# Moving weight-block preparation between stages, and two base blocks into a spare buffer, in a soft-routing expert matmul

## The chip, the cores and the metric

The kernel runs on one core of a Trainium2 chip. The metric is device time in microseconds (us) of one execution; lower is better. The core has TensorE (PE, matmuls; its weight loads are listed as PEld), VectorE (DVE), ScalarE (ACT), GpSimd (POOL) and SyncE (SP). In this kernel SyncE, ScalarE and GpSimd each issue DMA transfers from a queue of their own, and every engine works through its instructions in program order.

## The reference

Every token's row of x goes through all eight experts, and the results are summed with the softmax of the router's logits as weights:

```python
batch, seq, hidden, n_experts, expert_hidden = 16, 512, 512, 8, 2048
probs = softmax(router_logits)                     # (16, 512, 8)
for e in range(n_experts):
    output += probs[:, :, e:e+1] * np.matmul(x, expert_weights[e])
```

Inputs and output are float32. Seen as one matmul, the left matrix has 8192 rows (tokens) and 8 x 512 = 4096 columns, each x row scaled by its eight probabilities; the right matrix is the eight experts' weights under each other, 4096 x 2048.

## The kernel before, in words

The big matmul is done by Strassen's method in Winograd's form, at two levels everywhere and at a third level in part. At the outer level the tokens are taken in pairs of blocks of 256 rows (16 pairs, q = 0 to 15), the 4096 products' length in two halves (experts 0 to 3 and 4 to 7), and the 2048 output columns in two halves. So the weights are four blocks 11, 12, 21, 22, and seven kinds of product (P1 to P7) replace eight. Their right operands are 11 (P1), 21 (P2), T1 (P5), T2 (P6), T3 (P7), T4 (P4) and 22 (P3), where T1 to T4 are sums and differences of the four blocks. Each block has four parts, named by a pair kn: (0,0), (1,0), (1,1) and the "odd" part (0,1).

Each product is a smaller Winograd product of seven steps, and a step is one **slot**: 8 matmuls of 128 x 128 by 128 x 512, 1.73 us at full clock. A **stage** holds one product (7 slots) or two (14 slots, taken in turn). There are 56 stages. Where a stage has third-level work ("third"), the first four slots are replaced by 56 small matmuls, and the last two slots (12 and 13) of the stage before are held back and run inside it. Counting the program's matmuls against the trace gives the stages' starts:

| stages | what | first stage starts at, us |
|---|---|---|
| 0 to 6 | P1, q = 2 to 15, two a stage, all third | 38.9 |
| 7 to 14 | P2, two a stage; 8 to 12 third | 209.2 (stage 12: 323.4; 13: 350.3; 14: 374.4) |
| 15 | P5 for q = 0 and 1 | 398.6 |
| 16 | P6 for q = 0, alone | 422.8 |
| 17 to 30 | P6 for q and P5 for q + 1 | 438.9 (24.2 a stage) |
| 31 to 47 | P7, P4 | 777.3 |
| 48 to 55 | P3; 49 to 54 third | 1188.3 |

Before stage 0 the P1 products of q = 0 and 1 are done directly. Stage 4 starts at 130.7 and stage 5 at 154.0.

What an engine does beside the matmuls is placed by hooks: `at(stage, slot, make)` runs `make` just before that slot. DVE's longer work (left operands, sums of weights) is not run at once but put into one first-in-first-out list by `later(cost, make)`; `slack()` takes from it after each slot as far as a clock of planned costs allows, and `need(task)` takes everything up to that task. The left operands of stage s + 1 join this list after slot 0 of stage s. Results of matmul steps in PSUM are taken out by DVE or ACT right behind each step, in the same program order. In a third stage, two short DVE sums (line 735) stand between two groups of small matmuls, and TensorE waits for them.

Left operands are `z` tiles: x transposed (`xT`) times probabilities (`pT`). In P1 the x blocks of stages 3 to 6 are cast by GpSimd into tile `u` two stages ahead (`x_room`, `XBlock.begin`) and then transposed by SyncE's DMA (`XBlock.finish`).

Tiles come from pools: 15 buffers of 8 KB a partition for weights (`w`), 13 of 2 KB for half blocks of 128 x 512 float32 (`h`), 1 of 4 KB for `u`, 8 for `z`. A tile can be had only when the last use of its buffer is over, a DMA out of it included.

The parts that the change touches:

- `wedge(kn, e)` (one half e of part kn): GpSimd casts the half parts of 12 and 22 from float32 into one tile, DVE makes T1 = 11 - 12 and T2 = 22 + T1 of it, 128 x 2048 float16 each, and GpSimd sends both to DRAM for P5 and P6. There are six. `wedge_at(stage, slot, kn, e, then, apart)` places the first cast, the second `apart` slots later, and at `then` the two sums join DVE's list.
- The odd part: `cast_odd` casts it for 12, 11, 22 and 21 at the listed slots (two halves each); `odd_t` makes T1, T3 and T2 of it in place, three DVE sums of 128 x 4096, from (12, 5) on; `odd_t4` makes T4 from (15, 4) on, when the casts of 21 have landed.
- `Base`: P2 and P6 add to blocks that P1 left in DRAM (`kept`). `fetch(tn)` takes an `h` tile and loads one 128 x 512 block by SyncE. In P6 the result of P5 is then subtracted from it (`joined`, from slot 12 of the stage before), the matmul results are added in place, and GpSimd writes it out.

Of the kernel before, what the change touches and what calls it, by code (L numbers as in the profile page):

```python
# [31 lines left out]
def kernel(  # L32
# [8 lines left out]
    P = 128  # L41
    f16 = mybir.dt.float16
    f32 = mybir.dt.float32
    ADD, SUB, MUL = mybir.AluOpType.add, mybir.AluOpType.subtract, mybir.AluOpType.mult
# [5 lines left out]
    C = H // P  # L50
    HE = E // 2
    NB = 512
# [12 lines left out]
    zpool = ctx.enter_context(tc.tile_pool(name="zpool", bufs=8))  # L65
# [8 lines left out]
    def h_tile(shape, dtype):  # L74
        return hpool.tile(shape, dtype, name="h", tag="h")

    def half():
        return h_tile([P, NB], f32)
# [21 lines left out]
    def note(i):  # L100
        last[i.ins.engine] = i.ins
        if ordered[0]:
            tc.keep_in_program_order(i)

    def dve(i):
        last[i.ins.engine] = i.ins
        tc.keep_in_program_order(i)
# [3 lines left out]
    def tt(o, a, b, op):  # L111
        dve(nc.vector.tensor_tensor(out=o, in0=a, in1=b, op=op))  # L112
# [9 lines left out]
    def sp(o, i):  # L122
        note(nc.sync.dma_start(out=o, in_=i))

    def pool(o, i, **how):
        note(nc.gpsimd.dma_start(out=o, in_=i, **how))  # L126
# [32 lines left out]
    def kept_w(what, kn):  # L159
        if (what, kn) not in stored:  # L160
            stored[what, kn] = dram.tile([C, P, 2, NB] if what in TWOS else [P, K8, NB], f16, name="wd")
        kept_t = stored[what, kn]
        return kept_t.rearrange("a p b n -> p a b n") if what in TWOS else kept_t
# [122 lines left out]
    def third_weights(w, t, i):  # L286
        block = lambda k, n: w[:, ds(k * C, C), COLS[n]]
        x, y = ((block(0, 1), block(0, 0)), (block(1, 1), t[:, 0]), (block(1, 1), block(0, 1)),
                (block(1, 0), t[:, 1]))[i]
        tt(t[:, i], x, y, SUB)  # L290

    def new_t():
        return wpool.tile([P, 4, C, HQ], f16, name="t", tag="w")
# [116 lines left out]
    def need(task):  # L410
        if task is not None and not task.done:
            flush(task)
            clock["pe"] = max(clock["pe"], clock["dve"])

    def later(cost, make, first=False):
        t = Task(cost, make)
        (queue.appendleft if first else queue.append)(t)
        return t
# [144 lines left out]
    class Operand:  # L563
# [5 lines left out]
        def fetch(self):  # L569
            self.t = wpool.tile([P, 2, K8, HQ], f16, name="o", tag="w")  # L570
            note(nc.scalar.dma_start(out=self.t, in_=self.source))
# [78 lines left out]
    class Split:  # L650
# [10 lines left out]
        def make(self, p, i):  # L661
            if i == 0:
                self.t[p] = new_t()
            third_weights(self.right.op(p), self.t[p], i)
# [60 lines left out]
    def out_rows(q, odd, cols, tn):  # L725
        t, n = tn
        return out_f[ds((2 * q + odd) * HQ + t * HP, HP), ds(cols * NH + n * NB, NB)]

    def to_out(q, odd, cols, **how):
        return lambda tn, o: pool(out_rows(q, odd, cols, tn), o, **how)  # L730

    class Base:
# [2 lines left out]
        def __init__(self, source):  # L735
            self.source, self.t = source, {}

        def fetch(self, tn):
            self.t[tn] = half()
            sp(self.t[tn], self.source(tn))  # L740

        def __call__(self, tn):
# [8 lines left out]
    def at(stage, slot, make):  # L751
        hooks.setdefault((stage, slot), []).append(make)

    def add(*products):
        stages.append(products)
        return len(stages) - 1
# [4 lines left out]
    lefts, xs, ps_, bases = {}, {}, {}, {}  # L761
# [35 lines left out]
    def kept_rows(q):  # L797
        return lambda tn: kept[q][tn[1], ds(tn[0] * HP, HP), :]

    def product(r, q, **how):  # L800
        left, loads = left_of(r, q)
        lefts[r, q] = left
        p = None
        if r == 1:
            def sink(tn, o):
                pool(kept_rows(q)(tn), o)
            p = Product(right[1], left, sink)
        elif r == 2:
            if q >= 14:
                base = products[1, q].o.__getitem__  # L810
            else:
                base = bases[2, q] = Base(kept_rows(q))
            p = Product(right[2], left, to_out(q, 0, 0), base)
        elif r == 5:
            bases[6, q] = m1 = Base(kept_rows(q))
            m1.task = {}

            p = Product(right[5], left, to_out(q, 1, 0))
        elif r == 6:
            m1 = bases[6, q]  # L820

            def base(tn):
                need(m1.task[tn])
                return m1.t[tn]
            p = Product(right[6], left, to_out(q, 0, 1), base)
            if q in KEEP:
                left.kept = dram.tile([P, 2, K8, HQ], f16, name=f"kept_left_{q}")
        elif r == 7:
            if q < 14:
                base = bases[7, q] = Base(lambda tn: out_rows(q, 0, 1, tn))  # L830
            else:
                base = products[6, q].o.__getitem__
            p = Product(right[7], left, to_out(q, 1, 1), base)
        elif r == 4:
            p = Product(right[4], left, to_out(q, 1, 0, accum_op=ADD), products[7, q].o.__getitem__)
        else:
            p = Product(right[3], left, to_out(q, 0, 1, accum_op=ADD), **how)
        p.loads = loads
        products[r, q] = p
        return p  # L840
# [107 lines left out]
        for n in range(end, len(slots)):  # L948
            held.append(lambda n=n: one(n))

    def fetch_at(stage, slot, base, *tns):
        for tn in tns:
            at(stage, slot, lambda tn=tn: base.fetch(tn))


    for q in range(2, 16, 2):
# [1 line left out]
    forget(*range(0, 28, 2))  # L958
    rest = [14, 15] + list(range(14))
    for i in range(0, 16, 2):  # L960
        k = add(product(2, rest[i]), product(2, rest[i + 1]))
        for slot, tn in zip((8, 10, 12, 13), INNER):
            for q in rest[i:i + 2]:
                if q < 14:
                    fetch_at(k if tn == (1, 0) else k - 1, 3 if tn == (1, 0) else slot, bases[2, q], tn)
    xs.clear()
    k5 = add(product(5, 0), product(5, 1))
    add(product(6, 0))
# [20 lines left out]
    def joined(q, tn):  # L989
        m1 = bases[6, q]  # L990
        m1.task[tn] = later(0.61, lambda: tt(m1.t[tn], m1.t[tn], products[5, q].o[tn], SUB), True)

    for q in range(16):
        k = k5 + 1 + q
        duo = len(stages[k - 1]) == 2
        for slot, tn in zip((2, 4, 6, 8) if duo else (1, 2, 3, 4), INNER):
            fetch_at(k - 1, slot, bases[6, q], tn)
        for tn, where in zip(INNER, ((k - 1, 12), (k - 1, 13), (k - 1, 13), (k, 3)) if duo
                             else ((k - 1, 5), (k - 1, 6), (k - 1, 6), (k, 3))):
            at(*where, lambda q=q, tn=tn: joined(q, tn))  # L1000
        if q < 14:
            for slot, tn in zip((7, 9, 11, 17), INNER):
                fetch_at(k7 + q + 1 + slot // 14, slot % 14, bases[7, q], tn)
# [37 lines left out]
    b21, t1, t2, t3 = {}, {}, {}, {}  # L1041
# [11 lines left out]
    def sums_at(stage, slot, r, of, ps):  # L1053
        def go():
            if right[r].w is None:
                right[r].sums = right[r].build(of)
            for p in ps:
                right[r].queue_sum(right[r].sums, p)
        at(stage, slot, go)
# [1 line left out]
    sums_at(6, 6, 2, b21, (6,))  # L1061
    sums_at(6, 8, 2, b21, (7,))
    sums_at(6, 12, 2, b21, (4,))
    WEDGES = ((1,3,(1,11),4),(2,3,(2,11),4),(3,2,(3,9),4),(6,2,(6,11),4),(7,8,(8,7),4),(8,9,(9,9),4))
    for i, (kn, e) in enumerate((kn, e) for kn in ((0, 0), (1, 0), (1, 1)) for e in range(2)):
        wedge_at(*WEDGES[i][:2], kn, e, *WEDGES[i][2:])

# [3 lines left out]
    ODD = 0, 1  # L1071


    made = {}

    def cast_odd(q, e):
        if e == 0:
            made[q] = new_w()
        cast_w(q, ODD, e, made[q][:, ds(e * C, C), :])

    def odd_t():

        def make1():
            t1[ODD] = made[11]
            tt(t1[ODD], made[11], made[12], SUB)

        def make3():
            tt(made[12], made[22], made[12], SUB)
            pool(kept_w("t3", ODD), made.pop(12))

        def make2():
            t2[ODD] = made[22]
            tt(t2[ODD], made[22], t1[ODD], ADD)
        for make in (make1, make3, make2):
            later(2.2, make)

    def odd_t4():
        def make():
# [14 lines left out]
        return one(4, b[1, 0], b[1, 0], b[1, 1]) if all_ else sixth  # L1113

    last2 = k5 - 1
    for stage, slot, q, e in ((9, 9, 12, 0), (9, 13, 12, 1), (10, 4, 11, 0), (10, 9, 11, 1), (11, 2, 22, 0), (11, 7, 22, 1), (14, 8, 21, 0), (14, 12, 21, 1)):
        at(stage, slot, lambda q=q, e=e: cast_odd(q, e))
    at(12,5, odd_t)
    for i, kn in enumerate(((0, 0), (1, 1), (1, 0))):
        fetch_at_w(*(((11,8),(12,4),(13,0)))[i], t1, "t1", kn)  # L1120
# [229 lines left out]
```

## Time and profile before

| | us |
|---|---|
| median of 3 runs | 1365.48 |
| lowest, highest | 1364.68, 1372.43 |
| the profiled execution | 1371.11 |
| its span, first to last instruction | 1369.4 |
| TensorE busy | 1358.2 (99%) |
| DVE busy | 1154.2 (84%) |
| DMA queue of GpSimd, share of 16 engines | 56.5% |
| DMA queue of SyncE | 33.1% |
| DMA queue of ACT | 7.9% |

The profile is of one execution, which took 5.6 us more than the median. In the timeline a row is a run of like instructions: start, time to the end of the last, engine, line, what is written from what, how many, and in brackets how long the engine was idle before it and what ended that. In a table of stretches, PEclk is the share of its full clock that TensorE was granted, and the DMA share is the time of all packets over 16 engines' time; packets overlap, so it can pass 1.

### The profile page before, as it was taken

Reading aid. Unit: us, or ns where it says so; the run is one execution under the profiler, and the core shown is the slowest. Engines: PE = TensorE matmul, PEld = TensorE weight load, DVE = VectorE, ACT = ScalarE, POOL = GpSimd, SP = SyncE. Lnnn points to the kernel's source line nnn. Section 1 sums busy time; section 2 is a strip of 40 time slices with the busy share of each in tenths; the row PEclk is TensorE's granted clock in tenths of the full one; section 3 lists DMA queues with packets and bytes.
Section 4 is the critical chain, followed back from the end, with each engine's and each line's share of the span. In section 5 each row is a group of like instructions: output and inputs, shape, how many; then the busy total and the mean of one; then the engine's idle time right before and its main releaser. Section 6 shows DMA issues by size and latency. Waiting matters only on the chain.

```text
span 1369.4 us, 18641 instructions
## 1 busy us (share of the span) xinstructions
PE 1358.2 (99%) x6825; PEld 666.0 (49%) x6825; DVE 1154.2 (84%) x1429; ACT 204.5 (15%) x390; POOL 415.7 (30%) x650
## 2 busy tenths in 40 slices
PE   9999999999999999999999999999999999999998
PEld 4555555555444444444444444444444444456564
DVE  7987489988999888888878988888889797898873
ACT  3332221111011111111111100000000000123221
POOL 3133332231213243343323222232332422233232
PEclk9999999999999999999999999999999999999999
DMA  9999998999898999999999988889898979999896
GB/s 194 220 268 225 279 218 260 275 301 358 262 326 269 276 298 301 316 290 321 281 297 313 397 301 223 211 239 209 229 251 227 246 200 292 294 226 240 198 212 109
DMA packets 198811, 357.74 MB, mean 261 GB/s; under 512 B 53312, under 2 KB 90432, under 8 KB 194368
## 3 DMA queue, kind: packets, MB, share of 16 engines
q0 software_dynamic: 90448, 183.02, 56.5%
q1 hardware_dynamic: 100208, 133.56, 33.1%
q10 hardware_dynamic: 8064, 39.99, 7.9%
q8 instruction: 53, 0.87, 0.2%
q14 instruction: 38, 0.31, 0.1%
HBM read 218.92 MB, written 167.97 MB: 283 GB/s over the span
## 4 chain that ended last, share of the span: by engine, by line
PE 88%; issue 4%; DMA 3%; DVE 3%; POOL 1%; SPq 0%; POOLq 0%; ACT 0%; DVEq 0%
PE ps L132 88%; DMA out_dram<-h 2%; POOL out_dram L126 1%; DVE z L112 1%; DMA xT<-u 1%; DMA w<-in_expert_weights_dram 1%; DMA pT<-p_dram 1%; DVE h L112 0%; DVE t L112 0%; DVE u L112 0%; DVE s L112 0%; DVE d L112 0%; POOL wd L126 0%; DVE w L112 0%; POOL w L126 0%
## 5 line engine op out<-in xcount | busy, mean ns | idle before, releaser
L132 PE MATMUL ps<-w,z 128*128 128x512 f16 x5128 | 1094.5, 373 | 0.3 <-DMA w<-in_expert_weights_dram 0.3
L132 PEld LDWEIGHTS <-z 128*128 128x128 f16 x5272 | 516.1, 98 | 578.4 <-issue 5.1
L126 POOL DMA_DIRECT2D out_dram<-h x380 | 249.3, 662 | 710.2 <-ACT h L638 344.4
L112 DVE TENSOR_TENSOR h<-ps,h 128x512 f32<-128x512 f32 x415 | 283.4, 687 | 127.5 <-PE ps L132 114.5
L112 DVE TENSOR_TENSOR z<-xT,pT 128x2048 f16<-128x2048 f16 x216 | 261.5, 1218 | 23.8 <-DMA kept_left<-z 7.7
L132 PE MATMUL ps<-w,d 128*128 128x512 f16 x880 | 201.4, 382 | 2.2 <-DVE ps L112 2.2
L132 PEld LDWEIGHTS <-d 128*128 128x128 f16 x880 | 86.6, 98 | 103.8 <-issue 5.1
L112 DVE TENSOR_TENSOR z<-z,d 128x2048 f16<-128x2048 f16 x110 | 132.2, 1217 | 0.0
L112 DVE TENSOR_TENSOR w<-w 128x1024 f16<-128x1024 f16 (+2 forms) x100 | 108.1, 1091 | 13.6 <-DMA w<-in_expert_weights_dram 8.6
L638 ACT COPY h<-ps 128x512 f32<-128x512 f32 x64 | 37.5, 586 | 509.4 <-PE ps L132 461.6
L627 ACT COPY h<-ps 128x512 f32<-128x512 f32 x90 | 52.8, 587 | 273.8 <-PE ps L132 244.5
L112 DVE TENSOR_TENSOR d<-z 128x1024 f16<-128x1024 f16 x110 | 74.1, 687 | 1.5
L126 POOL DMA_DIRECT2D w<-in_expert_weights_dram x77 | 57.1, 753 | 44.4 <-DMA wd<-w 31.0
L624 ACT COPY h<-ps 128x512 f32<-128x512 f32 x90 | 51.6, 590 | 121.7 <-PE ps L132 97.5
L126 POOL DMA_DIRECT2D wd<-w x90 | 53.1, 605 | 43.9 <-DVE w L112 29.1
L126 POOL DMA_DIRECT2D kept<-h x56 | 30.9, 552 | 114.0 <-ACT h L627 85.0
L132 PEld LDWEIGHTS <-s 128*128 128x128 f16 x576 | 56.4, 98 | 10.6 <-issue 0.4
L132 PE MATMUL ps<-t,s 128*128 128x256 f16 x432 | 58.9, 273 | 0.1
L112 DVE TENSOR_TENSOR ps<-ps,d 128x256 f32<-128x256 f32 x72 | 30.2, 430 | 25.6 <-PE ps L132 25.5
L112 DVE TENSOR_TENSOR ps<-ps,h 128x512 f32<-128x512 f32 (+1 forms) x66 | 45.3, 688 | 4.7 <-PE ps L132 4.7
L112 DVE TENSOR_TENSOR h<-h 128x512 f32<-128x512 f32 (+2 forms) x69 | 45.1, 676 | 3.6 <-DMA out_dram<-h 3.5
L112 DVE TENSOR_TENSOR u<-xT,pT 128x2048 f16<-128x2048 f16 x38 | 46.3, 1218 | 0.0
(61 smaller groups left out, 354.8 us busy)
## 6 DMA issues: line engine op xcount, KB each, us to landing
out_dram<-h POOLq DMA_DIRECT2D x380, 256.0 KB, 7.3
pT<-p_dram SPq DMA_DIRECT2D x125, 256.0 KB, 7.0
h<-kept SPq DMA_DIRECT2D x120, 256.0 KB, 8.4
w<-wd ACTq DMA_DIRECT2D x25, 1024.0 KB, 10.6
xT<-x SPq DMA_DIRECT2D x77, 256.0 KB, 7.5
wd<-w POOLq DMA_DIRECT2D x76, 256.0 KB, 6.3
w<-in_expert_weights_dram POOLq DMA_DIRECT2D x35, 512.0 KB, 11.4
h<-out_dram SPq DMA_DIRECT2D x60, 256.0 KB, 5.4
```

Source lines behind the costliest of these rows:

```text
L112: dve(nc.vector.tensor_tensor(out=o, in0=a, in1=b, op=op))
L126: note(nc.gpsimd.dma_start(out=o, in_=i, **how))
L132: note(nc.tensor.matmul(ps, z, w, start=start, stop=stop, skip_group_check=True))
L624: act(nc.scalar.copy(o[tn], q if p == 5 else x))
L627: act(nc.scalar.copy(o[TN[p]], b if p == 2 else x))
L638: act(nc.scalar.copy(o[tn], b))
```

## The change

Four things change.

- The six wedges move. Old and new places (first cast; the sums join the list), in the order of the parts: (1,3; 1,11) to (0,4; 0,12); (2,3; 2,11) to (1,4; 1,12); (3,2; 3,9) to (6,3; 6,12); (6,2; 6,11) to (7,6; 7,13); (7,8; 8,7) to (8,6; 8,13); (8,9; 9,9) to (9,6; 9,13). The second cast stays four slots behind the first.
- The casts of the odd part of 21 go from slots 8 and 12 of stage 14 to slots 3 and 8.
- The three sums of `odd_t` are done in two halves each, six DVE operations of 128 x 2048 in the place of three of 128 x 4096.
- In stages 8, 10 and 12 of P2 the blocks (0,0) of both products, and in P6 for odd q from 1 to 13 the blocks (0,0) and (1,1), are loaded into the two halves of a tile of `u`'s buffer rather than into two `h` tiles.

```diff
-        def fetch(self, tn):
-            self.t[tn] = half()
+        def fetch(self, tn, pair=None):
+            if pair is None:
+                self.t[tn] = half()
+            else:
+                if not pair:
+                    two = zpool.tile([P, 2, NB], f32, name="r", tag="u", bufs=1)
+                    pair += [two[:, i] for i in range(2)]
+                self.t[tn] = pair.pop()
             sp(self.t[tn], self.source(tn))
...
     for i in range(0, 16, 2):
+        pair = [] if i // 2 in (1,3,5) else None
         k = add(product(2, rest[i]), product(2, rest[i + 1]))
...
-                    fetch_at(k if tn == (1, 0) else k - 1, 3 if tn == (1, 0) else slot, bases[2, q], tn)
+                    fetch_at(k if tn == (1, 0) else k - 1, 3 if tn == (1, 0) else slot, bases[2, q], tn,
+                             pair=pair if tn == (0, 0) else None)
...
         duo = len(stages[k - 1]) == 2
+        pair = [] if q in range(1, 14, 2) else None
         for slot, tn in zip((2, 4, 6, 8) if duo else (1, 2, 3, 4), INNER):
-            fetch_at(k - 1, slot, bases[6, q], tn)
+            fetch_at(k - 1, slot, bases[6, q], tn, pair=pair if tn in ((0, 0), (1, 1)) else None)
...
-    WEDGES = ((1,3,(1,11),4),(2,3,(2,11),4),(3,2,(3,9),4),(6,2,(6,11),4),(7,8,(8,7),4),(8,9,(9,9),4))
+    WEDGES = ((0,4,(0,12),4),(1,4,(1,12),4),(6,3,(6,12),4),(7,6,(7,13),4),(8,6,(8,13),4),(9,6,(9,13),4))
...
     def odd_t():
-
-        def make1():
+        halves = [ds(e * C, C) for e in range(2)]
+
+        def make1(h):
             t1[ODD] = made[11]
-            tt(t1[ODD], made[11], made[12], SUB)
-
-        def make3():
-            tt(made[12], made[22], made[12], SUB)
-            pool(kept_w("t3", ODD), made.pop(12))
-
-        def make2():
+            tt(t1[ODD][:, h], made[11][:, h], made[12][:, h], SUB)
+
+        def make3(h):
+            tt(made[12][:, h], made[22][:, h], made[12][:, h], SUB)
+            if h is halves[1]:
+                pool(kept_w("t3", ODD), made.pop(12))
+
+        def make2(h):
             t2[ODD] = made[22]
-            tt(t2[ODD], made[22], t1[ODD], ADD)
+            tt(t2[ODD][:, h], made[22][:, h], t1[ODD][:, h], ADD)
         for make in (make1, make3, make2):
-            later(2.2, make)
+            for h in halves:
+                later(1.14, lambda make=make, h=h: make(h))
...
-    for stage, slot, q, e in (..., (14, 8, 21, 0), (14, 12, 21, 1)):
+    for stage, slot, q, e in (...,(14,3,21,0),(14,8,21,1)):
```

More of the change, by code (lines that the diff above doesn't have):

```diff
@@ L949, in run, with fetch_at @@
             held.append(lambda n=n: one(n))
-    def fetch_at(stage, slot, base, *tns):
+    def fetch_at(stage, slot, base, *tns, pair=None):
         for tn in tns:
-            at(stage, slot, lambda tn=tn: base.fetch(tn))
+            at(stage, slot, lambda tn=tn: base.fetch(tn, pair))
     for q in range(2, 16, 2):
@@ L1115 @@
     last2 = k5 - 1
-    for stage, slot, q, e in ((9, 9, 12, 0), (9, 13, 12, 1), (10, 4, 11, 0), (10, 9, 11, 1), (11, 2, 22, 0), (11, 7, 22, 1), (14, 8, 21, 0), (14, 12, 21, 1)):
+    for stage, slot, q, e in ((9,9,12,0),(9,13,12,1),(10,4,11,0),(10,9,11,1),(11,2,22,0),(11,7,22,1),(14,3,21,0),(14,8,21,1)):
         at(stage, slot, lambda q=q, e=e: cast_odd(q, e))
```

## The prediction

> **What bounds the kernel now.** I read the page first, then the waits of TensorE alone, then the timeline around each of its two long waits, and last the table of stretches.
>
> ```profile
> span 1369.4 us, 18641 instructions
> ## 1 busy us (share of the span) xinstructions
> PE 1358.2 (99%) x6825; PEld 666.0 (49%) x6825; DVE 1154.2 (84%) x1429; ACT 204.5 (15%) x390; POOL 415.7 (30%) x650
> ```
>
> TensorE is busy for 1358.2 of 1369.4 us. No matmul is added or taken away, so the whole stake is what TensorE loses: 11.2 us of idle time, and any time in which its clock is low. The waits of TensorE name the large piece:
>
> ```profile
> PE ps L132 <- DVE ps L112: 5.3, 2, 3.1
> ```
>
> Two waits, 5.3 us together, the longer one 3.1. The other 5.9 us are the start, the tail and gaps too short to list, and nothing in the change touches those. The stretches just behind the two waits, and four stage-sized ones for later, show the clock:
>
> ```profile
> core 0: us, PE busy (x) PEld busy (x) DVE busy (x) ACT busy (x) POOL busy (x), PEclk, DMA share, GB/s
> 107.30:130.70 23.40, 23.40 (x138) 13.31 (x137) 17.94 (x23) 6.95 (x14) 9.82 (x16) 1.00 1.21 234
> 276.70:300.00 23.30, 23.30 (x137) 13.26 (x136) 20.96 (x30) 2.47 (x6) 8.11 (x14) 1.00 1.09 315
> 300.00:323.40 23.40, 23.40 (x137) 13.32 (x136) 21.14 (x30) 2.47 (x6) 5.80 (x11) 1.00 1.09 323
> 323.40:350.30 26.90, 26.90 (x154) 14.90 (x153) 22.74 (x28) 2.47 (x6) 4.44 (x9) 1.00 1.03 377
> 164.00:168.00 4.00, 2.01 (x11) 1.26 (x11) 1.90 (x3) 1.38 (x3) 0.00 (x0) 0.84 1.17 266
> 168.00:172.00 4.00, 4.00 (x16) 1.52 (x14) 0.29 (x1) 0.77 (x2) 0.00 (x0) 0.73 1.18 245
> 428.00:432.00 4.00, 3.42 (x11) 1.38 (x11) 3.60 (x6) 0.00 (x0) 0.00 (x0) 0.70 1.10 290
> 432.00:436.00 4.00, 4.00 (x18) 1.70 (x17) 2.04 (x3) 0.59 (x1) 0.56 (x1) 0.88 0.60 171
> ```
>
> After the first wait the granted clock is 0.84 and 0.73 over two stretches of 4 us: 4 x (0.16 + 0.27) = 1.72 us of work lost. After the second it is 0.70 and 0.88: 4 x (0.30 + 0.12) = 1.68 us. So each wait is paid twice, once as idle time and once as a slow clock.
>
> [...]
>
> The first wait is in the third-level part of stage 5:
>
> ```profile
> 164.37 1.23 DVE L112 TENSOR_TENSOR z<-xT,pT 128x2048 f16<-128x2048 f16 x1 [4.40 <-DMA xT<-u]
> 165.51 0.76 DVE L112 TENSOR_TENSOR ps<-ps,d 128x256 f32<-128x256 f32 x2
> 165.99 0.71 PE L132 MATMUL ps<-t,z 128*128 128x256 f16 x5 [3.09 <-DVE ps L112]
> ```
>
> DVE runs in order. It stood 4.40 us before a product for stage 6, because the transposed x (xT from u) had not landed, and the two short sums behind it were what TensorE needed. Back along that chain, the transposes and the casts of x into u:
>
> ```profile
> 151.39 10.03 SPq L463 DMA_TRANSPOSE xT<-u  x4
> ```
>
> ```profile
> 136.04 0.76 POOL L126 DMA_DIRECT2D w<-in_expert_weights_dram  x1 [3.67 <-DMA kept<-h]
> 137.41 0.54 POOL L126 DMA_DIRECT2D kept<-h  x1 [0.60 <-DMA kept<-h]
> 141.33 0.72 POOL L126 DMA_DIRECT2D u<-in_x_dram  x1 [3.38 <-DMA w<-in_expert_weights_dram]
> ```
>
> GpSimd (POOL) stood 3.67 + 0.60 + 3.38 = 7.65 us here, each time for an older transfer of its own queue to land. The stage before, from 107.3, has a DMA share of 1.21, the highest in the table: stage 3 carries a wedge and two casts of block 21.
>
> The second wait is in stage 16, which has one product instead of two, so that a late DVE has one slot (1.73 us) of grace there:
>
> ```profile
> 398.13 2.29 DVE L112 TENSOR_TENSOR w<-w 128x4096 f16<-128x4096 f16 x1 [1.26 <-DMA w<-wd]
> ...
> 410.62 6.82 DVE L112 TENSOR_TENSOR w<-w 128x4096 f16<-128x4096 f16 x3 [1.21 <-DMA w<-in_expert_weights_dram]
> ...
> 427.83 0.69 DVE L112 TENSOR_TENSOR ps<-ps,h 128x512 f32<-128x512 f32 x1
> ```
>
> ```profile
> 428.58 1.36 PE L132 MATMUL ps<-w,d 128*128 128x512 f16 x5 [2.18 <-DVE ps L112]
> ```
>
> From 410.62 to 427.83 DVE has no idle row at all. It is late by what it waited before: 1.26 us for a kept block t2, and 1.21 us for the second half of the odd block's cast 21, issued here:
>
> ```profile
> 397.70 0.77 POOL L126 DMA_DIRECT2D w<-in_expert_weights_dram  x1
> ```
>
> **The change part by part.** The profiled execution took 1371.1 us: the span of 1369.4 and 1.7 around it. The sum goes against that. The median shown is 1365.5, 5.6 less, so ordinary executions already lose less than the profiled one; against the median the gain must be smaller than the sum says.
>
> *Wedges.* A wedge is two casts, two DVE sums and two sends. DVE's work is a queue in order of arrival, and a wedge's sums stand between two stages' left operands. For the first, second, fourth and fifth wedge of the new list this place has a counterpart in the old one: (0,12) joins the queue where (1,11) did, since slots 12 and 13 run inside the next stage, (1,12) where (2,11) did, (7,13) where (8,7) did, (8,13) where (9,9) did; the third, (6,12), takes the place of (6,11). So in substance one wedge leaves stages 3 and 4, and one comes to stages 9 to 11. The prices:
>
> ```profile
> L112 DVE TENSOR_TENSOR w<-w 128x4096 f16<-128x4096 f16 x20 | 45.5, 2285 | 2.6 <-DMA w<-wd 1.3 <-DMA w<-in_expert_weights_dram 1.2
> ...
> L112 DVE TENSOR_TENSOR w<-w 128x2048 f16<-128x2048 f16 x16 | 19.5, 1219 | 4.6 <-DMA w<-in_expert_weights_dram 4.6
> ```
>
> ```profile
> q0 software_dynamic: 90448, 183.02, 56.5%
> ```
>
> DVE: 2 x 1.219 = 2.44 us. DMA: POOL's queue spends 56.5% of 1369.4 us, 774 us, on 183.02 MB, so 4.2 us a MB; a wedge moves four half blocks of 128 x 2048 f16 values, 0.52 MB each, 2.1 MB: 8.9 us of all 16 engines.
>
> Out of stages 3 and 4 go four POOL issues and those 8.9 us. The casts into u then need not stand 7.65 us; with half of it gone they come 3.8 us sooner, with all of it 7.65, against the 4.40 us that DVE waited. I take the wait as gone: -3.09 idle, -1.72 clock. Left as they were, both terms are 0.
>
> Into stages 9 to 11 go 2.44 us of DVE beside 23.3 - 20.96 = 2.3 and 23.4 - 21.14 = 2.3 us of idle time, so it is hidden if spread. And 8.9 us of DMA, where the share is already 1.09. This I cost at 0, with the other end as the second rival below.
>
> [...]
>
> The first wedge's casts move from stage 1 to stage 0, where POOL issues early and only small loads run. Cover: the rest of the old stage's time until DVE needs them. Gain or loss 0.
>
> *Odd block 21.* Its casts go from slots 8 and 12 of stage 14 to 3 and 8, so the second one is issued four slots sooner, 4 x 1.73 = 6.9 us against a wait of 1.21: that wait goes. The DVE chain behind it has no idle time, so it all arrives 1.21 us sooner at 427.83: idle 2.18 - 1.21 = 0.97. Does 0.97 us idle still cost clock? Between 0 and 1.68; 2.18 did, the gaps too short to list did not (1.00 in the rows of whole stages); I take 0, because 0.97 lies nearer to those gaps than to 2.18. Term: -1.21 - 1.68. The other side: the first cast now runs beside the fetch of t2 that DVE waits 1.26 us for at 398.13. If that fetch comes 1.2 us later, the term is 0 (first rival).
>
> *Sums in halves.* 3 x (2 x 1.219 - 2.285) = +0.46 us of DVE in stages 12 and 13, beside 26.9 - 22.74 = 4.2 us of idle time; the shorter pieces let accumulator sums in between. 0; uncovered +0.5.
>
> *Two base blocks in u's place.* Two more h buffers in effect. SyncE waits less for h; TensorE waits for none of it now. Gain 0. The cost is a rival below.
>
> Sum: 1371.1 - 3.09 - 1.72 - 1.21 - 1.68 = **1363.4 us**. All of the 8.7 us gone would be 1362.4.
>
> **The rivals.**
>
> *The t2 fetch moves with the cast.* The cast gains 1.21 us, the fetch loses as much, DVE stays late, and the second wait stays: 1371.1 - 4.8 = 1366.3.
>
> *Slower: the wedge in stages 9 to 11 makes the loads of stage 13 late.* DVE already waits there:
>
> ```profile
> 338.06 1.23 DVE L112 TENSOR_TENSOR z<-xT,pT 128x2048 f16<-128x2048 f16 x1 [2.45 <-DMA pT<-p_dram]
> 339.20 0.68 DVE L112 TENSOR_TENSOR h<-ps,h 128x512 f32<-128x512 f32 x1
> ```
>
> The sum at 339.20 ends at 339.9; TensorE needs its bank in slot 9 of stage 12, that is 5 slots before 350.3, 341.7. So from 1.8 us more of waiting for pT on, TensorE stands. If half of the wedge's 8.9 us falls on that load, it stands 2.7 us, with the clock 4.4: 1367.8; if all, 7.1 + 1.7 = 8.8: 1372.2. Above 2.1 us of new loss the time is over the median of before. For it: three stretches with shares of 1.09, 1.09 and 1.03. [...]
>
> *It doesn't do what it says.* Six casts of block 21 remain in stages 3 to 5, u's casts still stand, and the first wait stays: 1371.1 - 2.9 = 1368.2. Or ordinary executions have no such wait: 1365.5.
>
> *u holds SyncE up.* With one buffer, the next pair can be fetched only when both results of the last pair have been written out. In stage 21:
>
> ```profile
> 564.71 1.67 POOL L126 DMA_DIRECT2D out_dram<-h  x3 [1.24 <-DVE z L112]
> ```
>
> ```profile
> out_dram<-h POOLq DMA_DIRECT2D x380, 256.0 KB, 7.3
> ```
>
> ```profile
> 574.95 0.32 SPq L123 DMA_DIRECT2D h<-kept  x1
> ```
>
> The second of the pair, issued at 564.71, lands at about 572.0, and SyncE would stand until then; it stands until 574.95 today, for an h buffer. So little is lost; but if the fetch lands late for the subtraction in slot 12, DVE waits, and three such stages at 3 us and 1.7 of clock are 14 us: 1377.5.
>
> **How the numbers follow.** Forecast 1363.4 (1362 to 1365): 0.50. Second wait stays, 1366.3: 0.18. Late loads, 1367.8 to 1372.2: 0.20. Nothing done, 1365.5 to 1368.2: 0.07. u, up to 1377.5 and, with the late loads, beyond: 0.05. The range goes from 1361.0 (everything gone, 1362.4, less 1.4 for the spread of executions) to 1370.0, which leaves out the upper part of the late loads and u. A difference of 1% is 13.7 us, about what a measurement of this kernel tells from no change. Faster than 1351.8 isn't to be had, since TensorE's busy time less 3.4 of lost clock is 1354.8: 0.01. Slower than 1379.1 takes late loads and u together: 0.05. Within: 0.94.
>
> **What the changed profile would show.** Right: no wait for xT from u near 164; a granted clock of 1.00 there; casts into u of stage 4 with no stand of 3 us ahead of them; the three whole-block sums near 411 without a wait for the cast; TensorE's wait near 426 at about 1 us. Wrong: a DVE wait for pT of over 4 us near 338 with a new TensorE wait behind it; the wait for t2 near 398 grown past 2.4 us; the subtractions of P6 waiting for kept blocks. What makes the total wrong with each step right is that ordinary executions never had these waits, and the median then stays near 1365.

## The result, and the profile after

The changed kernel takes 1374.78 us (median of 11 executions, 1369.53 to 1382.96), the kernel before, beside it, 1364.94 (11 executions, 1363.87 to 1374.60). The ratio is 1.0067 (95% interval 1.0041 to 1.0092): 9.1 us slower, where 1363.4 was forecast and 1370.0 was the upper end of the range. The profiled execution took 1381.7 us, 10.6 more than the one of before. Each of the two is longer than the median of its kernel, by 6 to 7 us, so single stalls are read from the profiles and costs from the medians.

The page's first rows of the changed kernel, and the waits of its TensorE (total, times, longest, in us):

```profile
span 1380.0 us, 18624 instructions
...
PE 1360.6 (99%) x6825; PEld 666.2 (48%) x6825; DVE 1153.7 (84%) x1432; ACT 204.4 (15%) x390; POOL 415.2 (30%) x650
```

```profile
PE ps L132 <- DVE h L112: 7.2, 5, 3.5
PE ps L132 <- DVE ps L112: 6.5, 3, 3.3
```

There are as many matmuls as before, and now eight waits with 13.7 us where two with 5.3 us stood. The two old ones are gone: the casts into u and the transposes of stage 4 and 5 on the changed kernel's timeline, and its table of stretches (busy times, then PEclk, DMA share, GB/s):

```profile
141.65 1.46 POOL L126 DMA_DIRECT2D u<-in_x_dram  x2 [1.51 <-issue]
```

```profile
148.84 5.97 SPq L463 DMA_TRANSPOSE xT<-u  x4
```

```profile
core 0: us, PE busy (x) PEld busy (x) DVE busy (x) ACT busy (x) POOL busy (x), PEclk, DMA share, GB/s
164.00:168.00 4.00, 4.00 (x28) 2.56 (x27) 2.16 (x4) 0.96 (x3) 0.83 (x2) 1.00 1.08 356
168.00:172.00 4.00, 4.00 (x32) 2.99 (x31) 3.42 (x5) 2.09 (x4) 1.31 (x2) 1.00 1.10 254
...
425.30:428.70 3.40, 3.40 (x10) 1.22 (x9) 3.40 (x5) 0.58 (x1) 1.60 (x3) 0.51 1.01 417
599.50:602.90 3.40, 3.40 (x9) 1.22 (x8) 2.05 (x3) 0.00 (x0) 0.77 (x2) 0.50 1.05 370
```

POOL stands 1.51 us ahead of u's casts, not 3.38; the transposes take 5.97 us from first to last issue, not 10.03; and TensorE is busy throughout 164 to 172 at full clock, where it stood before. But half a clock is granted for 3.4 us at three other places, from 97.7, 425.3 and 599.5, each behind a new stall. (The row for the first stands in the last section.) I call them A, B and C.

**A, stages 1 and 2.** Timeline of the changed kernel, rows of SyncE, POOL, DVE and TensorE:

```profile
59.12 13.69 SPq L463 DMA_TRANSPOSE xT<-w  x4
```

```profile
54.69 0.77 POOL L126 DMA_DIRECT2D w<-in_expert_weights_dram  x1
```

```profile
76.85 1.23 DVE L112 TENSOR_TENSOR z<-xT,pT 128x2048 f16<-128x2048 f16 x1 [6.17 <-DMA xT<-w]
82.07 1.22 DVE L112 TENSOR_TENSOR z<-xT,pT 128x2048 f16<-128x2048 f16 x1 [4.00 <-DMA xT<-w]
```

```profile
89.06 2.76 PE L132 MATMUL ps<-w,z 128*128 128x512 f16 x16 [3.51 <-DVE h L112]
...
96.87 1.11 PE L132 MATMUL ps<-t,s 128*128 128x256 f16 x8 [2.45 <-DVE ps L112]
```

The first wedge's second cast goes out at 54.69, and SyncE's four transposes of x for stage 2 from 59.12 on, while it is still in flight (it lands at 65.77). DVE waits for them in program order, 6.17 and 4.00 us, and TensorE behind DVE.

**B, stages 14 to 16.** The same timeline: ACT's three fetches of t2, the first cast of block 21, DVE's sums of t2, and TensorE:

```profile
384.40 3.74 ACTq L180 DMA_DIRECT2D w<-wd  x3
```

```profile
381.11 0.76 POOL L126 DMA_DIRECT2D w<-in_expert_weights_dram  x1 [0.93 <-PE ps L132]
```

```profile
399.63 2.29 DVE L112 TENSOR_TENSOR w<-w 128x4096 f16<-128x4096 f16 x1 [1.99 <-DMA w<-wd]
...
406.79 2.29 DVE L112 TENSOR_TENSOR w<-w 128x4096 f16<-128x4096 f16 x1 [3.67 <-DMA w<-wd]
```

```profile
424.84 8.75 PE L132 MATMUL ps<-w,z 128*128 128x512 f16 x32 [2.60 <-DVE h L112]
```

No sum waits for the cast of block 21 any more, but two wait for t2, 5.66 us together against 1.26 before.

**C, stages 21 to 23.** SyncE's rows, the write of a pair's second result, DVE's subtraction and TensorE:

```profile
563.06 0.48 SPq L123 DMA_DIRECT2D kept_left<-z  x1
577.38 0.82 SPq L123 DMA_DIRECT2D r<-kept  x2
```

```profile
569.18 0.60 POOL L126 DMA_DIRECT2D out_dram<-r  x1
```

```profile
594.43 0.69 DVE L112 TENSOR_TENSOR h<-h 128x512 f32<-128x512 f32 x1 [3.33 <-DMA h<-kept]
```

```profile
598.65 5.30 PE L132 MATMUL ps<-w,d 128*128 128x512 f16 x16 [3.29 <-DVE ps L112]
```

Tile r is the pair in u's place. SyncE issues nothing from 563.54 to 577.38: it waits for u's only buffer, whose last reader is the write issued at 569.18, which lands at 577.23. SyncE issues in order, so the pair, two writes and the stage's last kept block go out in a bunch behind that stand, within 2.5 us. That last block, issued at 579.78, lands at 594.34, and DVE waits 3.33 us for it.

### The profile page after: what moved, and what is told of

Same layout as the page of the kernel before. It is cut to its first block, busy times and chain, and to the rows that moved or that the text cites. A ratio compares the mean times of both kernels' runs of the same rounds, so it can differ in the third digit from the quotient of the medians.

```text
span 1380.0 us, 18624 instructions
## 1 busy us (share of the span) xinstructions
PE 1360.6 (99%) x6825; PEld 666.2 (48%) x6825; DVE 1153.7 (84%) x1432; ACT 204.4 (15%) x390; POOL 415.2 (30%) x650
## 4 chain that ended last, share of the span: by engine, by line
PE 83%; DMA 9%; issue 4%; DVE 2%; POOL 1%; SPq 1%; POOLq 0%; ACT 0%; DVEq 0%
PE ps L132 83%; DMA wd<-w 2%; DMA xs<-in_x_dram 1%; DMA out_dram<-h 1%; DMA pT<-p_dram 1%; DMA xT<-w 1%; DMA xT<-xs 1%; DMA out_dram<-r 1%; DVE z L112 1%; SPq L463 1%; POOL out_dram L126 1%; DMA x<-xT 1%; DMA w<-in_expert_weights_dram 0%; DVE h L112 0%; POOL wd L126 0%
## 5 line engine op out<-in xcount | busy, mean ns | idle before, releaser
L126 POOL DMA_DIRECT2D out_dram<-h x360 | 238.4, 669 | 627.4 <-ACT h L638 261.1
L112 DVE TENSOR_TENSOR h<-ps,h 128x512 f32<-128x512 f32 x401 | 273.6, 685 | 128.0 <-PE ps L132 113.0
L638 ACT COPY h<-ps 128x512 f32<-128x512 f32 x51 | 29.9, 587 | 459.0 <-PE ps L132 433.8
L627 ACT COPY h<-ps 128x512 f32<-128x512 f32 x90 | 52.7, 585 | 286.0 <-PE ps L132 278.0
L126 POOL DMA_DIRECT2D wd<-w x90 | 52.8, 608 | 65.6 <-DVE w L112 52.0
L624 ACT COPY h<-ps 128x512 f32<-128x512 f32 x90 | 51.6, 590 | 122.2 <-PE ps L132 115.3
L126 POOL DMA_DIRECT2D w<-in_expert_weights_dram x77 | 57.5, 770 | 38.0 <-DMA wd<-w 29.1
L132 PEld LDWEIGHTS <-s 128*128 128x128 f16 x576 | 56.7, 99 | 13.7 <-issue 2.7
L112 DVE TENSOR_TENSOR h<-h 128x512 f32<-128x512 f32 (+3 forms) x55 | 36.2, 673 | 10.9 <-DMA h<-kept 10.7
L112 DVE TENSOR_TENSOR z<-z,u 128x2048 f16<-128x2048 f16 x34 | 41.3, 1214 | 0.1
```

What stands on the lines that cost most here:

```text
L132: note(nc.tensor.matmul(ps, z, w, start=start, stop=stop, skip_group_check=True))
L624: act(nc.scalar.copy(o[tn], q if p == 5 else x))
L627: act(nc.scalar.copy(o[TN[p]], b if p == 2 else x))
L638: act(nc.scalar.copy(o[tn], b))
```

## The experiments

The twelve kernels ran in three groups of four (e1 to e4, e5 to e8, e9 to e12), each group with the kernel before beside it: the first on one chip, the other two on another. So I compare by ratios to the kernel before, and 0.001 is 1.4 us. The intervals are 0.001 to 0.003 to each side, so differences under 2 us are weak. Between groups there is one more uncertainty: the median of the kernel before differs by 2 us (1366.37, 1364.34, 1364.69), while e4 and e9, the same kernel, differ by 0.6 (e9 was expected at 0.9975 and came out at 0.9977). All twelve compute the whole result.

| label | what stays of the change | median, us | before beside it | ratio (95%) |
|---|---|---|---|---|
| e1 | all but P6's pairs | 1371.72 | 1366.37 | 1.0033 (1.0013 to 1.0053) |
| e2 | all but the first two wedges | 1369.02 | 1366.37 | 1.0015 (0.9987 to 1.0044) |
| e3 | all but the casts of 21 | 1374.31 | 1366.37 | 1.0054 (1.0032 to 1.0076) |
| e4 | without these three parts | 1362.75 | 1366.37 | 0.9975 (0.9960 to 0.9990) |
| e5 | e4 and the first two wedges | 1366.23 | 1364.34 | 1.0014 (0.9998 to 1.0030) |
| e6 | e4 and the casts of 21 | 1364.23 | 1364.34 | 1.0007 (0.9992 to 1.0022) |
| e7 | e4 and P6's pairs | 1364.48 | 1364.34 | 1.0008 (0.9994 to 1.0021) |
| e8 | the last four wedges only | 1365.90 | 1364.34 | 1.0017 (1.0006 to 1.0028) |
| e9 | e4 again | 1362.20 | 1364.69 | 0.9977 (0.9967 to 0.9987) |
| e10 | e4 and P6's pairs in every fourth stage | 1362.27 | 1364.69 | 0.9975 (0.9964 to 0.9986) |
| e11 | e4 and the first wedge | 1364.41 | 1364.69 | 0.9997 (0.9983 to 1.0011) |
| e12 | the last four wedges and P2's pairs | 1362.65 | 1364.69 | 0.9979 (0.9964 to 0.9994) |

### Each part undone: e1, e2, e3, and all three: e4

My theory was that A, B and C have a cause each: the first two wedges' casts, the casts of block 21, P6's pairs in u. The rival was one common cause, the wedge that was added in stages 9 to 11, with the rest following from its delay.

```diff
 # e1
-            fetch_at(k - 1, slot, bases[6, q], tn, pair=pair if tn in ((0, 0), (1, 1)) else None)
+            fetch_at(k - 1, slot, bases[6, q], tn, pair=None)
 # e2
-    WEDGES = ((0,4,(0,12),4),(1,4,(1,12),4), ...
+    WEDGES = ((1,3,(1,11),4),(2,3,(2,11),4), ...
 # e3
-    ... (14,3,21,0),(14,8,21,1)):
+    ... (14,8,21,0),(14,12,21,1)):
 # e4: all of these
```

> The changed kernel with one part undone: the P6 base blocks (0,0) and (1,1) are all loaded into h tiles again (the P2 pairs in u stay). Theory (three separate causes): in the changed kernel SyncE stands from 563.5 to 577.4 in stage 22 because the pair's buffer u is handed back only when the last pair has been written out, DVE then waits 3.3 us for a kept block at 594.4, and TensorE loses 3.5 + 0.8 + 0.4 us idle and 1.7 us of clock behind it. Without the pairs that goes: no TensorE wait over 0.5 us between 540 and 650, the two earlier losses (near 85 to 94 and near 422) stay, and the time falls by some 4 to 6 us, to about 1369 to 1371. Rival (one common cause, the DMA queues filled by the wedge that now lies in stages 9 to 11, which makes all later work late): TensorE still waits near 595 and the time stays at 1375.

> The changed kernel with one part undone: the first two wedges are cast at (1,3) and (2,3) again, the other four stay at their new places. Theory: the casts of the first wedge in stage 0 slow the SyncE transposes of x for stage 2 (landed at 76.8 and 82.0, before the change at 61.6 to 65.5), DVE waits for xT, TensorE stands 3.7 and 2.6 us near 85 and 94 and loses 1.7 us of clock. With the wedges back the transposes land before 67, there is no TensorE wait before 400, and the time falls by some 5 to 8 us, to 1367 to 1370; the losses near 422 and 595 stay. Rival: the transposes are late for the weight casts of the start, not for the wedge, and TensorE still stands near 85.

> The changed kernel with one part undone: the two casts of the odd block 21 are at slots 8 and 12 of stage 14 again. Theory: in the changed kernel this cast takes a weight buffer ahead of the fetches of t2, so that the fetch of t2 (0,0) is issued at 384.4 instead of 371.1, t2 lands at 399.6 and 406.7 instead of 385.6 and 398.0, and DVE waits 1.99 and 3.67 us for it. With the casts back that fetch is issued before 378, DVE waits less than 2 us for t2, and TensorE's wait near 422 falls from 2.8 + 0.9 to 2.2 us or less; the time falls by 1 to 3 us, to 1372 to 1374. Rival (DVE is late in stages 13 to 15 for the wedge added in stages 9 to 11 and the sums of the odd block that came later for it): the fetch of t2 is still issued after 380 and TensorE's wait stays at 2.7 us or more.

> The three parts of the runs before undone together: what is left of the change is that the wedge of stages 3 and 4 has gone to stages 6 to 9 and the others behind it moved up, the odd sums in halves, and the P2 pairs in u. Theory: none of the long TensorE waits near 85, 94 and 595 is there, the old one near 163 is gone too, only the one near 426 is left; 1361 to 1364, faster than the kernel before by 1 to 4 us. Rival (the wedge in stages 9 to 11 is the common cause): 1368 or more, with waits behind stage 10.

Each stall went with its own part: e1 had none near 595, e2 none near 85 to 95, e3 none near 422. But the profiles alone don't separate them. e2's has no wait near 595 either, though its pairs in P6 remain; its two waits are 1.79 us up to 415.7 and 2.40 us up to 425.2. In e1 the waits that were expected to stay are 0.81 and 2.45 us near 87 and 95 and 0.95 us near 426 (3.51, 2.45 and 2.60 in the changed kernel), with no half clock. So the times have to decide as well. In ratio, e1 gives back 0.0034, e2 0.0052 and e3 0.0013 (4.6, 7.1 and 1.8 us); together 0.0099, against 0.0092 for all three at once. So they add up as far as these intervals can tell, and e3's 0.0013 by itself is within the noise. e4 keeps the wedge in stages 9 to 11 and has no long wait left, not even the one near 426 that was expected to stay; the common cause falls. Other misses: e1's time, 1371.72, lies over the 1369 to 1371 expected and e3's, 1374.31, over its 1372 to 1374, and in e3 t2's first fetch was still issued late, at 379.8.

### Each part alone: e5, e6, e7

> This is the version with all three parts back (1362.75 us) with the first two wedges alone in their early places again. Theory (the casts of stages 0 and 1 make the transposes for stage 2 land late): TensorE stands near 85 and 94 as in the changed kernel, 3.7 and 2.6 us, with a spell at half clock, and nothing near 422 and 595; the time is 4 to 8 us over that version, 1367 to 1371. Rival (the losses build on each other, and each alone is small): under 2 us over it, 1363 to 1364.5.

> This is the version with all three parts back, with the casts of block 21 alone in their early places. Theory (the cast takes a weight buffer ahead of the t2 fetches, which then issue 8 to 13 us later on ScalarE's queue and land late): t2's first fetch issues behind 379, DVE waits 2 to 4 us for it and TensorE 2 to 3 us near 414 to 422, with a spell at half clock: 1366 to 1369. Rival (the early cast costs nothing by itself; in the changed kernel the lateness came from what the early wedges and pairs had pushed back): no TensorE wait over 1 us there, 1362 to 1364.

> This is the version with all three parts back, with the pairs of P6 alone in u again. Theory (the fetch of the next pair waits on SyncE until both results of the last pair are out, and the bunch of fetches behind it lands late): TensorE stands about 3.5 us near 585 to 595 and up to 1 us in other stages of P6, with a spell at half clock: 1365.5 to 1369. Rival (u is late only because the kernel came late into that stage): no TensorE wait over 1 us behind 550, 1362 to 1364.

Against e9, which is e4 again in the third group (0.9977), they cost 0.0037, 0.0030 and 0.0031: 5.1, 4.1 and 4.2 us, with a sum of 13.4 us against 13.5 for the undone parts. Their medians themselves lie only 4.0, 2.0 and 2.3 us above e9's; the difference is that of the kernel before between the groups. So each part costs something (the three intervals lie clear of e9's), but the size is known to about 2 us only. All three times came out under what was expected, e5 at 1366.23 (1367 to 1371), e6 at 1364.23 (1366 to 1369), e7 at 1364.48 (1365.5 to 1369).

In a single profile the stalls are not always there: e5's execution took 1362.49 us and had none, though its median is 3.7 us more and its transposes were slower too. e7's has none near 585 to 595, and its longest is 1.04 us near 670; e6's is 1.94 us, without a spell at half clock. That an execution loses more or less as its transfers land later or sooner is my reading; one execution of each kernel was profiled, so it is not shown.

e6 corrects my mechanism for B. Its timeline:

```profile
373.07 0.76 POOL L126 DMA_DIRECT2D w<-in_expert_weights_dram  x1 [0.92 <-PE ps L132]
```

```profile
374.02 6.08 ACTq L180 DMA_DIRECT2D w<-wd  x3
```

```profile
395.52 2.29 DVE L112 TENSOR_TENSOR w<-w 128x4096 f16<-128x4096 f16 x1 [2.53 <-DMA w<-wd]
```

```profile
423.06 1.89 PE L132 MATMUL ps<-w,d 128*128 128x512 f16 x8 [1.94 <-DVE ps L112]
```

I had said that the cast takes a weight buffer ahead of the t2 fetches and so puts off their issue. In e6 the first is issued at 374.02, no later than in e4 (374.5). It lands late: 13.9 us after its issue, beside a cast that is in flight from 373.1 to 388.1. In e4 it took 9.6 us and in e9 7.9, where this cast goes out only at 384.9. The fetch that DVE then waits for is the second, issued at 376.26 and landed at 395.43: 19.2 us, against 14.2 in e4 and 14.1 in e9. Over the thirteen profiles other than before's, the second fetch takes 18.2 to 20.2 us in the four that have the early cast beside it and 13.7 to 18.2 in the nine others; the first takes 11.9 to 15.2 and 7.9 to 12.4. So the price is paid in the transfer. The late issue at 384.40 in the changed kernel is for the larger part the 8 us by which its TensorE is behind e6's there: the cast at 381.11 stands at 373.07 in e6.

### How u holds SyncE: e10

```diff
-        pair = [] if q in range(1, 14, 2) else None
+        pair = [] if q in range(1, 14, 4) else None
```

> The version with all three parts back, with pairs in u in every fourth stage of P6 only, so that a pair's two results have four stages to be written out before the next pair is fetched. Theory (SyncE is held by u's one buffer until the last pair is out): SyncE has no long stand ahead of these fetches, DVE no wait of 2 us or more for a kept block, TensorE none over 0.3 us behind 550: level with the version with all three parts back, 1361 to 1363.5. Rival (the order of the fetches and fewer h buffers at hand do it, not the hold): waits of DVE for kept blocks as with the pairs in every second stage, 1.5 to 3.5 us more.

It came out level with e9, as expected. The groups of DVE's subtractions by line, of the changed kernel, of e7 and of e10 (in each row the time at the end is idle time ahead of them and what ended it), and SyncE's waits for the pair's writes in the changed kernel and in e7:

```profile
L112 DVE TENSOR_TENSOR h<-h 128x512 f32<-128x512 f32 (+3 forms) x55 | 36.2, 673 | 10.9 <-DMA h<-kept 10.7
```

```profile
L112 DVE TENSOR_TENSOR h<-h 128x512 f32<-128x512 f32 (+3 forms) x55 | 36.2, 674 | 9.1 <-DMA h<-kept 9.0
```

```profile
L112 DVE TENSOR_TENSOR h<-h 128x512 f32<-128x512 f32 (+3 forms) x61 | 40.0, 673 | 0.1
```

```profile
SPq L123 <- DMA out_dram<-r: 40.3, 5, 13.7
```

```profile
SPq L123 <- DMA out_dram<-r: 33.3, 5, 13.6
```

With pairs in every second stage DVE waits 9 to 11 us for kept blocks, in every fourth 0.1 us. SyncE's 33 to 40 us of standing for the pair's writes has no row in e10. The order of the fetches and the number of h buffers, the rival, would have left part of DVE's wait.

But it is not that SyncE stands longer. Between 438 and 780 us it stands 40.1 us in all for results to be written in e7, 57.5 in e9, which has no pairs here, and 50.1 in e10: there the stands are for h buffers. What differs is what waits behind one. The same stage in e9 and in e7:

```profile
550.63 1.54 SPq L123 DMA_DIRECT2D h<-kept  x2
```

```profile
563.54 0.79 SPq L123 DMA_DIRECT2D r<-kept  x2
```

In e9 SyncE stands from 553.99 to 566.81, with only the stage's last kept block behind it (issued at 566.84). In e7 it stands from 549.76 to 563.54, ahead of the pair, and so these two blocks leave 13 us later. The last kept block leaves no later (565.38), but now in a bunch with the pair and two writes. It takes 12.4 us to land, against 5.4 in e9. Over all fourteen profiles this block takes 10.6 to 14.6 us in the four with these pairs and 4.9 to 6.6 in the ten without. In the changed kernel and in e7 DVE waits for it, 3.33 and 1.52 us.

### Which wedge: e11

```diff
-    WEDGES = ((1,3,(1,11),4),(2,3,(2,11),4), ...
+    WEDGES = ((0,4,(0,12),4),(2,3,(2,11),4), ...
```

> The version with all three parts back, with the first wedge alone early (casts in slots 4 and 8 of stage 0), the second wedge as before. Theory (the cast in slot 8 of stage 0 goes out just ahead of the transposes for stage 2 and shares the DMA rings with them): the transposes land at 67 to 75 as with both wedges early, not at 61 to 65; 2 to 5 us over the version with all three parts back. Rival (the second wedge's casts in stage 1 do it): the transposes land by 66 and the time is level.

The first wedge alone costs 0.0020 (2.7 us, by the medians 2.2), about half of the two. The median time to landing of the eight transposes out of `w` in the changed kernel and in e9; four of them are the ones in question:

```profile
xT<-w SPq DMA_TRANSPOSE x8, 8.9
```

```profile
xT<-w SPq DMA_TRANSPOSE x8, 4.1
```

Those four go out from 56.49 on in e11 and from 55.81 on in e9. In e11 they land at 70.6 to 78.2, in e9 at 62.4 to 68.4. Each takes 11.6 to 14.9 us in e11 and 13.0 to 14.7 in the changed kernel, against 3.6 to 6.6 in e9. So the first wedge's second cast, in flight beside them from 55.2 to 65.6 in e11, goes with most of the delay. That they share rings no trace shows; how a cast slows them (by a share of the DMA engines, or of something else) no run separates, and what the second wedge adds I did not separate either.

### What the last four wedges need: e8 and e12

```diff
 # e8: the kernel before with
+    WEDGES = ((1,3,(1,11),4),(2,3,(2,11),4),(6,3,(6,12),4),(7,6,(7,13),4),(8,6,(8,13),4),(9,6,(9,13),4))
 # e12: e8 and the pairs of P2 in u (pair=pair if tn == (0, 0) else None)
```

> This is the kernel before with the last four wedges moved and nothing else: no halves of the odd block's sums and no pairs in u. Theory (the wedges make the whole gain: u is free sooner for block 21's casts and the wait near 163 goes; halves and the pairs of P2 are worth nothing): 1361.5 to 1364, as the version with all three parts back, and no TensorE wait over 1 us. Rival (the halves remove the second wait, near 427): that wait of some 2 us stays, with a spell at half clock, 1365 to 1367.

> The version with all three parts back and the odd block's sums whole again, so that beside the last four wedges only the pairs of P2 are left of the change. Theory (the pairs of P2 let the kept blocks for stage 12 be fetched 8 us sooner and so take away the 4.2 us wait of DVE near 334 that the last four wedges alone had; the halves are worth nothing): no wait over 1 us of TensorE, level with the version with all three parts back. Rival (the whole sums make DVE late): TensorE stands 1 us or more between 325 and 345, with a spell at half clock, 2 to 4 us over it.

e8 refuted both of its hypotheses: the old waits near 163 and 427 were gone, and a new one came near 333. SyncE's fetch, DVE and TensorE in e8, and the same fetch in e12:

```profile
319.19 2.43 SPq L123 DMA_DIRECT2D h<-kept  x2
```

```profile
334.11 0.69 DVE L112 TENSOR_TENSOR h<-ps,h 128x512 f32<-128x512 f32 x1 [4.23 <-DMA h<-kept]
```

```profile
335.99 20.85 PE L132 MATMUL ps<-w,z 128*128 128x512 f16 x88 [2.50 <-DVE z L112]
```

```profile
310.70 1.73 SPq L123 DMA_DIRECT2D h<-kept  x2
```

In e12 P2's pairs let SyncE fetch these kept blocks 8.5 us sooner, and the wait is gone: 0.9979 against e8's 1.0017, 5.2 us by the ratios and 3.3 by the medians. In e8 the fetch goes out as soon as an older transfer, issued at 305.00, has landed at 319.11. The longest wait in e12 is 1.04 us, near 1169. The whole sums of the odd block, which e12 has again, make 0.0002 of difference to e9: the halves are worth nothing here.

## Why the prediction was wrong, by its steps

**First wait gone: right.** The casts into u no longer stand, and the 3.09 us and the clock loss near 164 are gone, in every version with the last four wedges.

**Second wait: gone, but not by the step that I named.** In e12 the casts of block 21 and the sums stand as before, and nothing waits near 427. There ACT's three t2 fetches are issued from 375.1 to 377.6; in the kernel before they spread over 16 us, as these rows of before and of e12 show:

```profile
371.13 16.12 ACTq L180 DMA_DIRECT2D w<-wd  x3
```

```profile
375.09 2.91 ACTq L180 DMA_DIRECT2D w<-wd  x3
```

In before's trace the first two name the same semaphore for their landing: the first, issued at 371.13, lands at 385.56, and the second goes out at 385.64. In the changed kernel they name different ones, and the second goes out at 386.53, while the first is in flight from 384.40 to 399.61. In e3, e6, e8 and e9 the three go out within 3.58, 6.08, 4.57 and 1.48 us, as in e12 within 2.91. So the second and third land at 398.0 and 406.6 in before and at 393.0 and 397.4 in e12, and the sums are early enough. Why the first two share a semaphore in the one kernel and not in the other, kernel.py does not say.

**"Gain or loss 0" for the first wedge's casts in stage 0: wrong, 5 to 7 us with the second wedge (A).** The step said that only small loads run there. But from about 56 us on the four transposes for stage 2 run there, and the step did not count what SyncE issues in those slots. Beside the casts they take two to three times as long (13.0 to 14.7 us in the changed kernel, 5.6 to 7.2 in before, 3.6 to 6.6 in e9). I compared where the wedges' sums join DVE's queue and found a counterpart for each; their casts, one stage sooner, have none.

**"Term: -1.21 - 1.68" for the casts of block 21: wrong sign, 2 to 4 us of loss (B).** The first rival (0.18) had the mechanism, the cast beside the t2 fetch. I let it eat up the gain at most; it took more, since the second wait needed no earlier cast to go.

**"Gain 0" for the pairs: wrong twice.** In P6 they cost 4 to 5 us (C), by the rival "u holds SyncE up", which got 0.05. Its mechanism is as written; what failed is "So little is lost". That step compared the end of the stand, 572.0 with pairs and 574.95 for an h buffer, and found no loss. The ends are indeed alike (563.54 in e7, 566.81 in e9), and the standing as a whole is hardly longer (51.7 us in the changed kernel between 438 and 780 us, 49.3 before). But the step did not ask what stands behind the waiting fetch: without pairs one kept block, with them three blocks and two writes, and all of it goes out in a bunch, so that the last block takes 10.6 to 14.6 us to land and not 4.9 to 6.6. In P2 the pairs gain 3 to 5 us: they are what keeps the wedge of stages 9 to 11 harmless.

**Late loads from that wedge (0.20): did not happen in the changed kernel,** where DVE has no wait over 0.7 us for a transfer between 110 and 399 us. The danger was real: e8 has it, on kept blocks instead of pT, and 2.50 us of TensorE instead of 2.7. What kept it off in the changed kernel was P2's pairs, as e12 against e8 shows, and these I had costed at 0.

**Size of the good part.** The sum took 7.7 us off one profiled execution. Against medians, e4 and e9 gain 0.0025 and 0.0023, about 3.3 us. The prediction said that ordinary executions lose less than the profiled one, and then let the forecast rest on the profiled one. e4 and e9, the change without its three bad parts, nevertheless take 1362.75 and 1362.20, close to the 1363.4 that was forecast for the whole. Partly this is luck: the sum starts about 6 us above the median and takes about 4 us more off than was gained. Partly it is a floor: 1362.4 was the prediction's time with both waits and their loss of clock gone, and e9's executions lie between 1361.5 and 1363.2. With -3.3 us for the good part and the parts alone at +5.1, +4.1 and +4.2, the change comes to +10.1 us; measured were 9.1.

## What to carry to other kernels

When an instruction that starts a transfer is moved, list what every other queue has in flight in the new place, not only what its engine does there. A tile with one buffer, fetched from SyncE's queue, held all that was queued behind it here, for 13.8 us (563.54 to 577.38 in the changed kernel), until the last reader's write had landed, so look up when that reader runs in the program with the change, and which fetches are queued behind the one that waits. That a wait of the same length was there before says little, when it stood ahead of less. An edit that seems worth nothing can be the cover of another: undo the parts one by one and together, and add each alone, before keeping or dropping the whole.

## What the runs showed of the hardware

Half a clock was granted in spells of one length. Seven of them lie inside the spans of before (from 166.74 and 429.57), of the changed kernel (97.70, 425.38 and 599.46), of e2 (424.83) and of e8 (336.43), each with a PEclk of 0.50 over 3.41 to 3.42 us. In the traces of before and of the changed kernel they are 3.413 us long, and their starts lie 262.83 us apart in the one, 327.68 and 174.08 in the other: 77.0, 96.0 and 51.0 times that length. So I cut each profile into stretches of this length, from the start of a spell on and back (of the one at the profile's end, where none lies inside the span). Four such stretches of the changed kernel, then two of e2 and two of e6:

```profile
core 0: us, PE busy (x) PEld busy (x) DVE busy (x) ACT busy (x) POOL busy (x), PEclk, DMA share, GB/s
84.04:87.45 3.41, 1.48 (x12) 1.19 (x13) 3.37 (x6) 1.30 (x4) 0.00 (x0) 1.00 1.15 257
87.45:90.87 3.42, 1.81 (x9) 0.86 (x9) 3.42 (x5) 0.00 (x0) 0.54 (x1) 1.00 1.37 167
94.28:97.69 3.41, 0.96 (x9) 0.73 (x8) 3.41 (x5) 0.58 (x1) 3.07 (x6) 1.00 1.04 414
97.69:101.11 3.42, 3.42 (x18) 2.38 (x17) 3.35 (x6) 1.10 (x3) 0.41 (x1) 0.50 1.08 222
```

```profile
421.42:424.83 3.41, 1.38 (x7) 0.51 (x6) 3.38 (x5) 0.00 (x0) 0.94 (x2) 1.00 1.03 336
424.83:428.25 3.42, 3.04 (x8) 1.09 (x8) 3.18 (x4) 0.00 (x0) 0.00 (x0) 0.50 0.94 245
```

```profile
420.54:423.95 3.41, 1.47 (x8) 0.60 (x7) 3.38 (x4) 0.00 (x0) 0.00 (x0) 1.00 1.08 237
423.95:427.37 3.42, 3.42 (x17) 1.53 (x16) 3.42 (x6) 0.59 (x1) 0.00 (x0) 1.00 1.01 261
```

The longest stall, 3.51 us up to 89.06, is split between two stretches, with 1.48 and 1.81 us of work left in them: no loss of clock. The shorter one of 2.45 us lies in one stretch with 0.96 us of work: half a clock in the next. Half a clock came behind seven stretches, with 0.75 and 1.24 us of work in before, 0.96, 0.81 and 0.80 in the changed kernel, 1.38 in e2 and 0.91 in e8. None came behind seven others, with 1.48 and 1.81 us in the changed kernel, 1.83 in e1, 1.69 and 1.98 in e3, 1.47 in e6 and 1.73 in e11. So a stall cost its own length, and behind those first seven stretches another 1.7 us, half of 3.41. Its length alone did not decide: 2.45 us cost clock here and 3.51 us did not. These are fourteen cases of one kernel; what another does they don't show.

In the traces of before and of the changed kernel every transfer of SyncE and ACT names a semaphore for its landing. In each, 555 of the 563 have an earlier one ahead of them on theirs, and none of the 555 goes out before that one has landed; 52 in before and 43 in the changed kernel follow within 0.15 us of that landing. So in these two kernels a transfer could be held by an older one that it has nothing to do with, as I take the second t2 fetch of before to have been: it went out 14.5 us behind the first, against 2.1 us in the changed kernel.
